# Hybrid retention and differential attention on one core: attention in one step per product, a fixed rotation of raw weight slots, and two weight sums made by adding DMAs

## The chip, the cores and the metric

The kernel runs on 1 core of one Trainium2 chip. The metric is the device time of one execution in microseconds; a kernel's time is the median of its runs. Engines are named as the profile names them: PE (TensorE, matmuls), DVE (VectorE), ACT (ScalarE), POOL (GpSimd) and SP (SyncE, which here only issues DMAs). L813 means line 813 of the kernel's file. One execution of each kernel is recorded by the hardware profiler; all rows below come from it.

## The reference, cut to what matters

```python
u = rms_norm(h, g_norm)                      # h: 16 meta tokens + 512 tokens, D_MODEL 2048
proj = u @ w_in                              # 2048 x 8192, float32
rq, rk, rv, rgate, dq, dk, dv, dgate = jnp.split(proj, offs, axis=-1)
# 8 heads of each kind, 128 wide
r = retention(rq, rk, rv, valid)             # chunk-causal, decay by distance
r = head_layer_norm(r, g_ret) * jax.nn.silu(rgate)
d = diff_attention(dq, dk, dv, valid, lam)   # softmax(q0 k0) - lam * softmax(q1 k1), then v
d = head_rms_norm(d, g_diff) * (1.0 - lam_init) * jax.nn.silu(dgate)
y = jnp.concatenate([r, d], axis=-1) @ w_out # 2048 x 2048
return rms_norm(h + y, final_norm_g)
```

All of it is float32. The kernel splits each float32 operand in a high and a low part and makes one product of three matmuls (high x high, high x low, low x high).

## The kernel before

**Stages.** From 0 to about 100 us the rows of x are normed and transposed and the first six column groups are projected one by one. From about 100 to 806 us the other 58 column groups of w_in are projected two at a time, in 29 pairs such as (dv, dk) or (rq, rg) of one head, and the attention of the heads runs between them. From 806 us on the output projection and the last norm follow.

**A pair and its seven products.** A pair takes two column groups ka and kb, the 2048 rows of w_in in two halves, and the tokens in two halves. That is a 2 x 2 block product, done with seven block products P1 to P7 in place of eight, which needs sums of raw weight pieces. A raw piece is 128 x 1024 float32, 512 KB: b11 and b21 are the two halves of ka, b12 and b22 those of kb. `ORDER` is P3, P7, P1, P6, P2, P5, P4. Each product needs its piece split: ACT casts it to `wh` (L785), DVE makes `wl` from it (L796); both are prepared two products ahead, with three buffers each. PE then runs 24 matmuls (L813). Between the splits four sums per pair are made in the raw pieces, two on DVE (L799, L801) and two on POOL (L803, L804). PSUM banks p3, v, x, y collect the products; ACT copies p3, v and x out of three rotating banks (`snap`, L825) and DVE adds (L829).

**Attention in steps.** `ret_task` (retention of a head) and `diff_task` (differential attention of a head) are generators; `step()` takes every task in the list one `yield` further, and `run_pair` calls it at chosen places between the products. A diff task takes, for four query blocks and two softmaxes, scores (PE, L590, L596), score plus distance and row maximum (DVE, L604), the maximum times the slope (L606), the exponential (ACT, L607), and combines the two (L613 to L616); then transposes (PE, L629), splits and the product with v. ACT loads its table anew when it goes from SiLU to the exponential or back (ACT_TABLE_LOAD). A step of the retention is one block of scores s_r, times the decay table (L552), split (L556, L557), and one block back its product with v, `o_r` (L526 to L528).

**The end of a head, `finish`.** The head's rows get a norm factor in hops: squares, one matmul `ms` (PE, L463), a copy of its first row (ACT, L464), a DMA of that row to a column `mc` (SP, L467), four small POOL instructions (L469 to L472), a DMA to DRAM `rd` (L474) and a broadcast back into `sq` (L476); then DVE multiplies the head `oc` by it (L479), by the gain and the SiLU gate (L480), and the head is split into `mxh` and `mxl` and both are written to DRAM (L490), to be read back before the output projection.

**What sets the order.** A pass that places instructions before the run fixes each engine's order; engines then run their lists in order and wait at semaphores, and SP and POOL do so for the DMAs they issue as well. Heads 1 to 6 take their pairs in the order (rv, rk), (rq, rg), (dv, dk), (dq, dg); head 7 takes dv, dk and dq, dg first. Raw pieces come from a pool of five buffers (`wr`), loaded by SP in w_in's own layout, 512-byte rows.

Of the kernel before, what the change touches and what calls it, by code (L numbers as in the profile page):

```python
# [15 lines left out]
P = 128  # L16
# [23 lines left out]
def hymba_kernel(ctx: ExitStack, tc: tile.TileContext, x, meta, norm_g, w_in, w_out, g_ret, g_diff,  # L40
# [14 lines left out]

    def pj(name):
        return ps.tile([P, 512], F32, tag="pj", bufs=3, name=name)
# [85 lines left out]
    mt = ap.tile([4 * META, 512], F32, tag="s2k", bufs=3, name="mt")  # L143
# [304 lines left out]
    def finish(po, col, T, gate, nm):  # L448
        oc = ap.tile([P, L], F32, tag="s2k", bufs=3, name=f"oc_{nm}")[:, :SEQ]
        vec.tensor_scalar(oc, po, OMAX, -OMAX, op0=ALU.min, op1=ALU.max)  # L450

        sq = ap.tile([P, L], F32, tag="s2k", bufs=3, name=f"sq_{nm}")[:, :SEQ]
        sr = ap.tile([P, L], F32, tag="s2k", bufs=3, name=f"sr_{nm}")[:, :SEQ]
# [13 lines left out]
        nc.sync.dma_start(out=mc, in_=sq[0:1, :].rearrange("o (p j) -> o p j", j=4))  # L467
        rc = sm.tile([P, 4], F32, tag="rc", name=f"rc_{nm}")
# [4 lines left out]
        rd = dr.tile([P, 4], F32, tag="rd", name=f"rd_{nm}")  # L473
        nc.sync.dma_start(out=rd, in_=rc)  # L474
        bc = sq
        nc.sync.dma_start(out=bc, in_=rd.rearrange("p j -> (p j)").rearrange("(o n) -> o n", o=1)  # L476
                          .broadcast_to([P, SEQ]))
        yield
        vec.tensor_tensor(out=oc, in0=oc, in1=bc, op=ALU.mult)  # L479
        vec.scalar_tensor_tensor(oc, oc, gcol[:, col:col + 1], T[gate], op0=ALU.mult, op1=ALU.mult)  # L480
        if col in heads_mix:
            hi, lo = heads_mix[col]
        else:
            hi, lo = (ap.tile([P, SEQ], F32R, tag="r2k", bufs=4, name=f"mx{t}_{nm}") for t in "hl")
        act.copy(out=hi, in_=oc)  # L485
        vec.tensor_tensor(out=lo, in0=oc, in1=f(hi), op=ALU.subtract)
        if col not in heads_mix:
            spilled[col] = dr.tile([P, 2, SEQ], F32, tag=f"mx{col}", bufs=1, name=f"mx{col}")
            for j, t in enumerate((hi, lo)):
                nc.sync.dma_start(out=spilled[col][:, j, :], in_=f(t))  # L490
# [38 lines left out]

    def ret_task(h, T):  # L530
        nm = f"r{h}"
        tab = ap.tile([P, 576], F32, tag="tab", name=f"tab{h}")
        nc.sync.dma_start(out=tab, in_=decay_tab[h])
        vh, vl = v_rows(T["rv"], nm, True)
# [3 lines left out]
        state["scores"] = state.get("scores", 0) + 5  # L538
        t0s = [0, 64, 192, 320, 448]
        prev = None  # L540
        for i in range(6):
            if i < 5:
# [8 lines left out]
                pf = ap.tile([P, L], F32, tag="s2k", bufs=3, name=f"pf_{nm}_{i}")  # L551
# [22 lines left out]
    def diff_task(h, T):  # L574
        nm = f"d{h}"
        vh, vl = T["d_rows"] if "d_rows" in T else v_rows(T["dv"], nm, False)
        slope = 2.0 ** -(h + 1)
        state["scores"] = state.get("scores", 0) + 4
        aa = []
        for b in range(4):  # L580
            w = 2 * 72 + P * b
            zz = sm.tile([P, 2], F32, tag="zz", name=f"zz_{nm}_{b}")
            pp = []

            for s in range(2):
# [26 lines left out]
            rr = sm.tile([P, 2], F32, tag="rr", name=f"rr_{nm}_{b}")
            vec.reciprocal(rr, zz)  # L613
            vec.tensor_tensor(out=rr[:, 1:2], in0=rr[:, 1:2], in1=neglam, op=ALU.mult)
            vec.tensor_scalar(pp[1], pp[1], rr[:, 1:2], None, op0=ALU.mult)  # L615
            vec.scalar_tensor_tensor(pp[0], pp[0], rr[:, 0:1], pp[1], op0=ALU.mult, op1=ALU.add)  # L616
            aa.append(pp[0])
            yield

# [75 lines left out]
    def put_dk(src):  # L695

        a = kbuf[0]
        for (d1, cols), (d2, _) in zip(*(both_parts(a[:, i, :]) for i in range(2))):
            act.copy(out=d1, in_=src[:, :, cols])
            vec.tensor_tensor(out=d2, in0=src[:, :, cols], in1=f(d1), op=ALU.subtract)  # L700
        return spread_dk()

    def spread_dk():
        a, b = kbuf
        for rows in (slice(0, DH), slice(DH, P)):
            nc.sync.dma_start(out=f(b[rows]), in_=f(a[DH:]))
        nc.sync.dma_start(out=f(a[DH:]), in_=f(a[:DH]))
        return [(t[:, 0, :], t[:, 1, :]) for t in kbuf]
# [15 lines left out]
    def sums_of_u():  # L724
# [3 lines left out]
        for k in range(0, 8, 2):  # L728
# [7 lines left out]
            def out(i, t):  # L736
                act.copy(out=sums[i][0][:, sl, :], in_=t)
                vec.tensor_tensor(out=sums[i][1][:, sl, :], in0=t, in1=f(sums[i][0][:, sl, :]), op=ALU.subtract)

            c = whole("fc", [t[k // 4] for t in uc], slice(k % 4, k % 4 + 2), "s2k", 3)  # L740
            d = whole("fd", ud, sl, "s2k", 3)
            vec.tensor_tensor(out=d, in0=c, in1=d, op=ALU.add)
            out(1, d)
# [44 lines left out]
    def prepare_lo(i):  # L788
# [27 lines left out]
    def run_pair(n, T):  # L816
# [38 lines left out]
        if keys:  # L855
            step()
# [11 lines left out]
        step()  # L868
        run(5, y, True)
# [3 lines left out]
        if ka in ("rq", "dq"):  # L873
# [3 lines left out]
            act.activation(T[kb], T[kb], AF.Silu)  # L877
        else:
# [3 lines left out]
            if kb == "rk":  # L882
                T[kb] = [kbuf[0][:, i, :] for i in range(2)]
                for (d1, cols), (d2, _) in zip(*(both_parts(t) for t in T[kb])):
                    act.activation(d1, s37[:, :, cols], AF.Copy, scale=K_SCALE)
                    vec.scalar_tensor_tensor(d2, s37[:, :, cols], K_SCALE, f(d1), op0=ALU.mult, op1=ALU.subtract)
            else:
                T[kb] = put_dk(s37)
        run(6, v, True)

        if keys:
            for d, cols in key_parts(vT, 1):
                add(d, su2[:, cols], v[:, cols])
# [43 lines left out]
    load_pair(0)  # L937
# [13 lines left out]
    prepare_hi(0)
    prepare_lo(0)
    prepare_hi(1)
    prepare_lo(1)
# [13 lines left out]
    for ks in kpairs:  # L968
        for k in list(range(KT))[ks]:
            if k in spilled:  # L970
                for j, t in enumerate(heads_mix[k]):
                    nc.sync.dma_start(out=f(t), in_=spilled[k][:, j, :])

# [146 lines left out]
```

## Time and profile before

| | us |
|---|---|
| median of 3 runs | 1033.93 (1033.39 to 1037.14) |
| the profiled execution, its own time | 1036.45 |
| its span in the trace | 1034.4 |
| PE busy | 964.7 (93% of the span) |
| DVE busy | 824.0 (80%) |
| ACT busy | 538.7 (52%) |
| POOL busy | 242.7 (23%) |
| DMA queue of SP, share of the 16 DMA engines | 42.2% |

The time is the whole execution; the span runs from the first to the last instruction of the trace, 2.05 us less here. Busy shares are means over stages that differ: a window of the span tells which engine works and which waits there.

### The profile page before, as it was taken

How to read it: one execution, taken by the hardware profiler on the slowest of the kernel's cores; microseconds unless marked ns; L12 is line 12 of the kernel's file. 1: busy time of each engine (PE TensorE's matmuls, PEld its weight loads, DVE VectorE, ACT ScalarE, POOL GpSimd, SP SyncE). 2: the span in 40 equal slices, each digit the busy share in tenths (PEclk: the TensorE clock that was granted, in tenths of full speed). 3: DMA queues.
4: the chain of work that ended last, by engine and by line, in shares of the span. 5: the costliest groups of instructions: out<-in, count | busy, mean ns of one | idle time of the engine just before them, and what ended most of it. 6: DMA issues, size and time to landing. Idle time of an engine off the chain costs nothing.

```text
span 1034.4 us, 18382 instructions
## 1 busy us (share of the span) xinstructions
PE 964.7 (93%) x7215; PEld 921.6 (89%) x7215; DVE 824.0 (80%) x1332; ACT 538.7 (52%) x979; POOL 242.7 (23%) x169
## 2 busy tenths in 40 slices
PE   6999988999999999899999999999994999799997
PEld 6999988999999999899999999999983988588896
DVE  6698869899989998999899989989996754334432
ACT  6454565565656564646565656565654443223322
POOL 4453131132233213321332133233220200000001
PEclk8999999999999999999999999999997999999998
DMA  9512533353235334543643264226443496143304
GB/s 269 158 43 73 125 93 103 82 155 114 82 97 152 107 109 116 139 121 87 140 134 98 82 156 113 83 82 156 113 113 102 161 385 212 50 126 96 122 1 163
DMA packets 166405, 127.03 MB, mean 123 GB/s; under 512 B 9712, under 2 KB 145008, under 8 KB 165808
## 3 DMA queue, kind: packets, MB, share of 16 engines
q1 hardware_dynamic: 165744, 124.04, 42.2%
q10 hardware_dynamic: 576, 1.84, 0.5%
q8 instruction: 56, 0.92, 0.4%
q14 instruction: 29, 0.24, 0.1%
HBM read 107.77 MB, written 11.57 MB: 115 GB/s over the span
## 4 chain that ended last, share of the span: by engine, by line
PE 54%; DVE 21%; DMA 9%; issue 6%; POOL 6%; ACT 4%; SPq 0%; POOLq 0%; DVEq 0%; ACTq 0%
PE y L526 6%; PE y L527 5%; PE y L528 5%; DVE wl_P L796 5%; PE y_rqrg L813 4%; PE x_dvdk L813 3%; PE x_dqdg L813 3%; DMA mc_r<-sq_r 2%; PE x_rqrg L813 2%; PE y_dvdk L813 2%; PE v_rqrg L813 2%; DMA sq_r<-rd_r 2%; PE v_dvdk L813 2%; DVE p_d L615 2%; PE y_rvrk L813 2%
## 5 line engine op out<-in xcount | busy, mean ns | idle before, releaser
L785 ACT CAST wh_P<-b 128x1024 fp32r<-128x1024 f32 x203 | 212.7, 1049 | 147.9 <-DVE mx_d L606 30.3
L796 DVE TENSOR_TENSOR wl_P<-b,wh_P 128x1024 fp32r<-128x1024 f32 x203 | 260.3, 1284 | 13.0 <-ACT wh_P L785 11.0
L803 POOL TENSOR_TENSOR b<-b,b 128x1024 f32<-128x1024 f32 x29 | 69.9, 2412 | 406.1 <-DVE b L799 301.7
L104 DVE TENSOR_TENSOR wl<-wr,wh 128x1024 fp32r<-128x1024 f32 (+1 forms) x40 | 49.8, 1252 | 69.3 <-ACT wh L103 69.2
L804 POOL TENSOR_TENSOR b<-b,b 128x1024 f32<-128x1024 f32 x29 | 76.8, 2649 | 105.5 <-DVE wl_P L796 32.5
L103 ACT CAST wh<-wr 128x1024 fp32r<-128x1024 f32 (+1 forms) x40 | 40.8, 1029 | 88.7 <-PE y L528 70.1
L607 ACT ACTIVATE p_d<-p_d,mx_d 128x144 f32<-128x144 f32 (+3 forms) x64 | 36.6, 572 | 31.7 <-DVE mx_d L606 31.1
L799 DVE TENSOR_TENSOR b<-b,b 128x1024 f32<-128x1024 f32 x29 | 35.5, 1223 | 0.6
L629 PE MATMUL at_d<-ident,p_d 128*128 128x128 f32 (+1 forms) x112 | 23.1, 275 | 13.3 <-DVE p_d L616 12.9
L801 DVE TENSOR_TENSOR b<-b,b 128x1024 f32<-128x1024 f32 x29 | 35.2, 1214 | 0.1
L813 PE MATMUL x_dqdg<-uah,wh_P 128*128 128x256 f32 x128 | 32.2, 290 | 3.0 <-ACT s_dqdg L825 3.0
L1049 POOL TENSOR_SCALAR rs<-ssq,pre 128x1 f32<-128x1 f32 x4 | 1.9, 486 | 136.1 <-ACT jk L1007 136.1
L813 PE MATMUL x_dqdg<-ual,wh_P 128*128 128x256 f32 x128 | 31.2, 282 | 0.0
L526 PE MATMUL y<-wh,mix_s3h 128*128 128x512 f32 (+1 forms) x64 | 23.6, 382 | 6.3 <-ACT mix_s3h L485 5.1
L813 PE MATMUL x_dvdk<-uah,wh_P 128*128 128x264 f32 x112 | 28.5, 284 | 0.0
L813 PE MATMUL x_dvdk<-ual,wh_P 128*128 128x264 f32 x112 | 28.4, 284 | 0.0
L813 PE MATMUL x_rvrk<-uah,wh_P 128*128 128x264 f32 x112 | 28.4, 285 | 0.0
L813 PE MATMUL x_rvrk<-ual,wh_P 128*128 128x264 f32 x112 | 28.2, 285 | 0.0
L629 PEld LDWEIGHTS at_d<-ident,p_d 128*128 128x128 f32 (+1 forms) x112 | 12.8, 126 | 17.3 <-DVE p_d L616 14.8
L813 PEld LDWEIGHTS x_dqdg<-uah,wh_P 128*128 128x128 f32 x128 | 24.1, 188 | 4.2 <-ACT s_dqdg L825 4.2
L526 PE MATMUL y<-wh,mix_s2h 128*128 128x512 f32 (+1 forms) x80 | 27.8, 348 | 0.0
L528 PE MATMUL y<-wh,mix_al 128*128 128x512 f32 (+1 forms) x80 | 27.8, 348 | 0.0
(567 smaller groups left out, 3550.5 us busy)
## 6 DMA issues: line engine op xcount, KB each, us to landing
b<-in_w_in_dram SPq DMA_DIRECT2D x116, 512.0 KB, 4.6
wr<-in_w_out_dram SPq DMA_DIRECT2D x32, 512.0 KB, 4.1
kbuf<-kbuf SPq DMA_DIRECT2D x24, 264.0 KB, 4.9
wr<-in_w_in_dram SPq DMA_DIRECT2D x12, 512.0 KB, 8.5
tab<-in_decay_tab_dram SPq DMA_DIRECT2D x8, 288.0 KB, 4.3
sq_r<-rd_r SPq DMA_DIRECT2D x8, 256.0 KB, 3.6
sq_d<-rd_d SPq DMA_DIRECT2D x8, 256.0 KB, 4.2
mx<-mxh_r SPq DMA_DIRECT2D x7, 256.0 KB, 3.7
```

Source lines behind the costliest of these rows:

```text
L103: act.copy(out=hi, in_=raw)
L104: eng.tensor_tensor(out=lo, in0=raw, in1=f(hi), op=ALU.subtract)
L526: pe.matmul(o, ah, bh, start=start, stop=False)
L527: pe.matmul(o, ah, bl, start=False, stop=False)
L528: pe.matmul(o, al, bh, start=False, stop=stop)
L607: act.activation(p, p, AF.Exp, bias=mx, scale=slope, accum_out=zz[:, s:s + 1])
L629: pe.transpose(at[:n, b * P - q0:(b + 1) * P - q0], aa[b][:, kc:kc + n], ident)
L785: act.copy(out=hi, in_=raw_w[n][SOURCE[pn]])
L796: vec.tensor_tensor(out=lo, in0=w[SOURCE[pn]], in1=f(hi), op=ALU.subtract)
L803: pool.tensor_tensor(out=w["b12"], in0=w["b12"], in1=w["b11"], op=ALU.subtract)
L804: pool.tensor_tensor(out=w["b11"], in0=w["b21"], in1=w["b22"], op=ALU.subtract)
L813: pe.matmul(o, w_[:, kt, :], u[lo][:, kt, c0:], start=not add and w_ is wh and kt == 0 and lo == 0, stop=w_ is wl and kt == 7, skip_group_ ...
```

## The change

- **Pairs.** Heads 1 to 7 all take (dv, dk), (dq, dg), (rv, rk), (rq, rg), so the retention of a head runs beside the next head's dv, dk and dq, dg, and the diff attention beside its own head's rv, rk and rq, rg. `ORDER` ends P4, P5; P4 goes to the bank of v. The three PSUM banks are chosen by name.
- **Steps.** One `step()` per product, in `run` itself (two in pair 1 and the first three products of pair 2). `finish` has seven more yields; the combining of a diff block comes one block later, and its scaling by the second softmax's factor goes from DVE to ACT. The maximum is taken as a minimum of the negated scores, so L606's multiplication goes. Rows of v and the copies of k are tasks of their own.
- **Weights.** w_in is laid out on the host so that a piece is one contiguous block. Five raw slots rotate by a fixed table. Per pair five plain loads (t, b22, b11, b21, t1; t1 is b11's data again) and two adding DMAs from POOL: t += half 1 of kb, t1 += half 0 of kb. DVE makes t += b11 behind P7's split and t += b21 behind P6's. POOL's sums go. Signs are folded into the sums of u, the scale of SiLU and that of k.
- **Spilled heads.** They are written whole, in one DMA, and split when they are read back.

```diff
-    ORDER = ("P3", "P7", "P1", "P6", "P2", "P5", "P4")
+    ORDER = ("P3", "P7", "P1", "P6", "P2", "P4", "P5")
...
-        ps_ = ps_[3:] if h == 0 else ps_[2:] + ps_[:2] if h == HEADS - 1 else ps_
+        ps_ = ps_[3:] if h == 0 else ps_[2:] + ps_[:2]
...
-        if pn == "P3":
-            vec.tensor_tensor(out=w["b22"], in0=w["b22"], in1=w["b12"], op=ALU.subtract)
-        elif pn == "P7":
-            vec.tensor_tensor(out=w["b22"], in0=w["b22"], in1=w["b11"], op=ALU.add)
-        elif pn == "P1":
-            pool.tensor_tensor(out=w["b12"], in0=w["b12"], in1=w["b11"], op=ALU.subtract)
-            pool.tensor_tensor(out=w["b11"], in0=w["b21"], in1=w["b22"], op=ALU.subtract)
+        if pn == "P7":
+            vec.tensor_tensor(out=w["t"], in0=w["t"], in1=w["b11"], op=ALU.add)
+        elif pn == "P6":
+            vec.tensor_tensor(out=w["t"], in0=w["t"], in1=w["b21"], op=ALU.add)
...
+    slots = [{"t": 0, "b22": 1, "b11": 2, "b21": 3, "t1": 4}]
+    for n in range(len(pair_list)):
+        p_ = slots[n]
+        slots.append({"t": p_["b22"], "b22": p_["b11"], "b11": p_["b21"], "b21": p_["t"], "t1": p_["t1"]})
...
+    def loads(n, j):
+        m = n + 1
+        if j == 0:
+            more(n, "t1", 0)
+        elif j == 1:
+            more(m, "t", 1)
+            load(m, "b22")
+        elif j == 3:
+            load(m, "b11")
+        elif j == 4:
+            load(m, "b21")
+        elif j == 5:
+            load(m, "t1")
+        elif j == 6:
+            load(m + 1, "t")
+    def more(n, b, half):
+        if n < len(pair_list):
+            h, _, kb = pair_list[n]
+            pool.dma_start(out=raw_w[n][b].rearrange("p (k n) -> p k n", n=P), in_=w_piece(kb, h, half), accum_op=ALU.add)
+    SOURCE = {"P7": "t", "P3": "b22", "P1": "b11", "P6": "t", "P2": "b21", "P5": "t1", "P4": "t"}
...
         def run(j, o, more=False):
+            loads(n, j)
             prepare_hi(i0 + j + 2)
             prepare_lo(i0 + j + 2)
+            step()
+
+            if n == 1 or n == 2 and j < 3:
+                step()
             product(i0 + j, o, keys, more)
...
+        def combine(b, zz, pp):
+            rr = sm.tile([P, 2], F32, tag="rr", name=f"rr_{nm}_{b}")
+            vec.reciprocal(rr, zz)
+            vec.tensor_tensor(out=rr[:, 1:2], in0=rr[:, 1:2], in1=neglam, op=ALU.mult)
+            act.activation(pp[1], pp[1], AF.Copy, scale=rr[:, 1:2])
+            yield
+            vec.scalar_tensor_tensor(pp[0], pp[0], rr[:, 0:1], pp[1], op0=ALU.mult, op1=ALU.add)
+            aa.append(pp[0])
...
-                vec.tensor_tensor_reduce(shape(p), shape(dist[:, 384 - P * b:]), sp, op0=ALU.add, op1=ALU.max,
-                                         scale=1.0, scalar=-3e38, accum_out=mx)
-                vec.tensor_scalar(mx, mx, -slope, None, op0=ALU.mult)
-                act.activation(p, p, AF.Exp, bias=mx, scale=slope, accum_out=zz[:, s:s + 1])
+                vec.tensor_tensor_reduce(shape(p), shape(dist[:, 384 - P * b:]), sp, op0=ALU.add, op1=ALU.min,
+                                         scale=-slope, scalar=3e38, accum_out=mx)
+                act.activation(p, p, AF.Exp, bias=mx, scale=-1.0, accum_out=zz[:, s:s + 1])
...
+        yield
+        yield
         rc = sm.tile([P, 4], F32, tag="rc", name=f"rc_{nm}")
...
         rd = dr.tile([P, 4], F32, tag="rd", name=f"rd_{nm}")
+        yield
         nc.sync.dma_start(out=rd, in_=rc)
+        yield
         bc = sq
...
         yield
+        yield
         vec.tensor_tensor(out=oc, in0=oc, in1=bc, op=ALU.mult)
```

POOL's list before, in head 2 (`b` are raw pieces, `rc` and `mc` a head's norm factor):

```order
L804 TENSOR_TENSOR b_7_3256<-b_7_3258,b_7_3252 128x1024
L803 TENSOR_TENSOR b_8_3589<-b_8_3589,b_8_3591 128x1024
L469 TENSOR_SCALAR rc_d_3644<-mc_d_3642 128x4
L470 TENSOR_TENSOR rc_d_3644<-rc_d_3644,mhalf 128x4
L471 TENSOR_SCALAR mc_d_3642<-mc_d_3642 128x4
L472 TENSOR_TENSOR rc_d_3644<-rc_d_3644,mc_d_3642 128x4
L804 TENSOR_TENSOR b_8_3591<-b_8_3593,b_8_3587 128x1024
```

and after, in head 1 (`t_3` is t1 of pair 3, the other two are t and t1 of pair 4):

```order
L835 DMA t_3_2155<-in_w_in_dram 128x1024
L835 DMA t_2191<-in_w_in_dram 128x1024
L479 TENSOR_SCALAR rc_d_2019<-mc_d_1982 128x4
L480 TENSOR_TENSOR rc_d_2019<-rc_d_2019,mhalf 128x4
L481 TENSOR_SCALAR mc_d_1982<-mc_d_1982 128x4
L482 TENSOR_TENSOR rc_d_2019<-rc_d_2019,mc_d_1982 128x4
L835 DMA t_4_2469<-in_w_in_dram 128x1024
```

The sums of 128x1024 are gone; an adding DMA stands at most of their places, and a head's factor still stands between two of them.

DVE's list before, where the diff attention of heads 6 and 7 meet (`oc_d` is head 6, the scores and the gate `sg` head 7):

```order
L616 SCALAR_TENSOR_TENSOR p_d_2_0_9746<-p_d_2_0_9746,rr_d_2_9759,p_d_2_1_9754 128x400
L479 TENSOR_TENSOR oc_d_9732<-oc_d_9732,sq_d_9734 128x512
L604 ISA p_d_3_1_9863,mx_d_3_1_9864<-dist,s_d_3_1_9858 128x528
L604 ISA mx_d_3_1_9864 128x1
L480 SCALAR_TENSOR_TENSOR oc_d_9732<-oc_d_9732,gcol,sg_dg_8943 128x512
L606 TENSOR_SCALAR mx_d_3_1_9864<-mx_d_3_1_9864 128x1
L829 TENSOR_TENSOR sg_dg_9564<-s_dqdg_9438,s_dqdg_9335 128x256 x2
```

and after, where those of heads 0 and 1 meet:

```order
L601 SCALAR_TENSOR_TENSOR p_d_1_0_2291<-p_d_1_0_2291,rr_d_1_2333,p_d_1_1_2299 128x272
L492 TENSOR_TENSOR oc_d_1918<-oc_d_1918,sq_d_1920 128x512
L631 ISA p_d_2_1_2349,mx_d_2_1_2350<-dist,s_d_2_1_2346 128x400
L631 ISA mx_d_2_1_2350 128x1
L631 ISA p_d_3_0_2396,mx_d_3_0_2397<-dist,s_d_3_0_2391 128x528
L631 ISA mx_d_3_0_2397 128x1
L493 SCALAR_TENSOR_TENSOR oc_d_1918<-oc_d_1918,gcol,sg_dg_1555 128x512
L597 RECIPROCAL rr_d_2_2386<-zz_d_2_2337 128x2
L885 TENSOR_TENSOR sg_dg_2223<-s_dqdg_2081,s_dqdg_1959 128x256 x2
```

The multiplication that waits for the broadcast of the earlier head stands ahead of the later head's scores and gate in both; the heads are 0 and 1 now, and in heads 6 and 7 it no longer does.

DVE's list before, where head 3's diff attention ends:

```order
L440 TENSOR_TENSOR p_str<-pf_r_4_6130,p_str 16x64
L796 TENSOR_TENSOR wl_P_6295<-b_16_6061,wh_P_6293 128x1024
L479 TENSOR_TENSOR oc_d_6007<-oc_d_6007,sq_d_6009 128x512
L480 SCALAR_TENSOR_TENSOR oc_d_6007<-oc_d_6007,gcol,sg_dg_5232 128x512
L450 TENSOR_SCALAR oc_r_6282<-o_r_5973 128x512
```

and after:

```order
L571 TENSOR_TENSOR pl_r_1_5449<-pf_r_1_5446,ph_r_1_5448 128x448
L492 TENSOR_TENSOR oc_d_5242<-oc_d_5242,sq_d_5244 128x512
L885 TENSOR_TENSOR su_dvdk_5480<-s_dvdk_5427,pj_dvdk_5429 128x264
L855 TENSOR_TENSOR wl_P_5486<-t_13_5236,wh_P_5484 128x1024
L566 TENSOR_TENSOR pf_r_2_5493<-s_r_2_5489,tab_5391 128x320
```

Before, the retention's last score block is already behind DVE when the multiplication comes; after, it stands between the second and the third block of the retention (`pl_r_1`, `pf_r_2`) of the same head, beside the next head's (dv, dk).

## Rows read from the trace of the kernel before

**Rows 1.** The page's first part: busy us, share, instructions of PE.

```profile
PE 964.7 (93%) x7215; PEld 921.6 (89%) x7215; DVE 824.0 (80%) x1332; ACT 538.7 (52%) x979; POOL 242.7 (23%) x169
```

**Rows 2.** Windows of the span: length, busy us of each engine, granted clock, DMA.

```profile
0.00:200.00 200.00, 181.24 (x1424) 175.33 (x1425) 160.98 (x277) 109.43 (x213) 64.03 (x51) 0.98 0.43 121
200.00:700.00 500.00, 482.17 (x3882) 473.33 (x3881) 472.23 (x747) 299.88 (x538) 141.01 (x86) 1.00 0.43 113
700.00:781.00 81.00, 76.58 (x623) 75.01 (x622) 77.61 (x129) 48.04 (x89) 21.67 (x11) 1.00 0.52 131
781.00:806.00 25.00, 10.25 (x51) 8.47 (x50) 12.84 (x36) 8.99 (x19) 1.85 (x4) 0.66 0.25 76
786.80:803.80 17.00, 6.41 (x27) 5.71 (x27) 6.63 (x20) 6.12 (x13) 0.32 (x2) 0.50 0.23 69
```

**Rows 3.** Waits of PE from 200 to 700 us: total, times, longest.

```profile
PE at_d L629 <- DVE p_d L616: 6.7, 5, 2.0
PE s_d L590 <- DVE mx_d L604: 5.3, 4, 1.4
PE x_dqdg L813 <- ACT s_dqdg L825: 2.6, 3, 1.4
```

**Rows 4.** Timeline of the last head: start, length, engine, [idle before, releaser].

```profile
782.02 0.47 PE L463 MATMUL ms_d<-sh_d,ones 128*128 128x512 f32 x1 [0.77 <-DVE mx_d L604]
...
793.61 0.69 DVE L479 TENSOR_TENSOR oc_d<-oc_d,sq_d 128x512 f32<-128x512 f32 x1 [4.37 <-DMA sq_d<-rd_d]
...
796.99 1.28 ACT L877 ACT_TABLE_LOAD   x1
...
799.23 0.59 PE L813 MATMUL y_rvrk<-s2h,wh_P 128*128 128x264 f32 x1 [9.34 <-ACT s_rvrk L825]
799.62 0.42 PE L813 MATMUL y_rvrk<-s2l,wh_P 128*128 128x264 f32 x1
799.84 0.42 PE L813 MATMUL y_rvrk<-s2h,wh_P 128*128 128x264 f32 x1
```

**Rows 5.** POOL's second sum by line (busy, mean ns), and one in the timeline.

```profile
L804 POOL TENSOR_TENSOR b<-b,b 128x1024 f32<-128x1024 f32 x29 | 76.8, 2649 | 105.5 <-DVE wl_P L796 32.5
...
771.55 2.40 POOL L804 TENSOR_TENSOR b<-b,b 128x1024 f32<-128x1024 f32 x1 [5.18 <-DVE wl_P L796]
771.78 2.44 DVE L693 SCALAR_TENSOR_TENSOR dq_h<-su_dqdg,dq_h 64x256 fp32r<-64x256 f32 x1
774.26 0.42 DVE L693 SCALAR_TENSOR_TENSOR dq_l<-su_dqdg,dq_l 64x256 fp32r<-64x256 f32 x1
```

**Rows 6.** Groups of instructions by line: busy us, mean ns | idle before.

```profile
L796 DVE TENSOR_TENSOR wl_P<-b,wh_P 128x1024 fp32r<-128x1024 f32 x203 | 260.3, 1284 | 13.0 <-ACT wh_P L785 11.0
...
L606 DVE TENSOR_SCALAR mx_d<-mx_d 128x1 f32<-128x1 f32 x64 | 8.3, 147 | 0.2
...
L877 ACT ACT_TABLE_LOAD x7 | 9.0, 1283 | 0.1
```

**Rows 7.** Timeline of PE inside one product, at the full clock.

```profile
442.66 0.28 PE L813 MATMUL y_rvrk<-s1h,wh_P 128*128 128x264 f32 x1
442.79 0.28 PE L813 MATMUL y_rvrk<-s1l,wh_P 128*128 128x264 f32 x1
```

**Rows 8.** DMA issues: queue, count, KB each, median us to landing.

```profile
b<-in_w_in_dram SPq DMA_DIRECT2D x116, 512.0 KB, 4.6
...
wr<-in_w_in_dram SPq DMA_DIRECT2D x12, 512.0 KB, 8.5
...
hr_dh<-in_x_dram SPq DMA_DIRECT2D x1, 1024.0 KB, 16.2
...
mc_r<-sq_r SPq DMA_DIRECT2D x8, 2.0 KB, 4.1
```

**Rows 9.** Timeline in a head whose finish runs beside POOL's sums.

```profile
395.12 0.39 PE L463 MATMUL ms_d<-sh_d,ones 128*128 128x512 f32 x1
...
410.28 0.69 DVE L479 TENSOR_TENSOR oc_d<-oc_d,sq_d 128x512 f32<-128x512 f32 x1 [2.08 <-DMA sq_d<-rd_d]
```

More of the change, by code (lines that the diff above doesn't have):

```diff
@@ L54, in f @@
         return t.bitcast(F32)
+    state = {"n": 0, "pieces": 0, "ring": -1, "scores": 0, "pj": -1}
     def pj(name):
-        return ps.tile([P, 512], F32, tag="pj", bufs=3, name=name)
+        state["pj"] = (state["pj"] + 1) % 3
+        return ps.tile([P, 512], F32, tag=f"pj{state['pj']}", name=name)
     def pm(name):
@@ L481, in finish @@
         if col in heads_mix:
-            hi, lo = heads_mix[col]
+            split(oc, *heads_mix[col])
         else:
[L484 to L490, printed above, removed]
+            spilled[col] = dr.tile([P, SEQ], F32, tag=f"mx{col}", bufs=1, name=f"mx{col}")
+            yield
+            nc.sync.dma_start(out=spilled[col], in_=oc)
     def v_rows(vT, nm, centre):
@@ L611, in diff_task @@
             state["scores"] -= 1
[L612 to L617, printed above, removed]
+            late = (b, zz, pp)
             yield
+        for _ in combine(*late):
+            pass
+        yield
         tiles = [(META, 0, 0, 4), (P, 16, 0, 0), (P, 144, P, 1), (P, 272, 2 * P, 2), (P, 400, 3 * P, 3)]
@@ L661, in scores_done @@
     def scores_done():
-        while state.get("scores", 0):
+        while state["scores"]:
             step()
@@ L698, in put_dk, with spread_task @@
         for (d1, cols), (d2, _) in zip(*(both_parts(a[:, i, :]) for i in range(2))):
[L699 to L703, printed above, removed]
+            act.activation(d1, src[:, :, cols], AF.Copy, scale=-1.0)
+            vec.scalar_tensor_tensor(d2, src[:, :, cols], -1.0, f(d1), op0=ALU.mult, op1=ALU.subtract)
+        tasks.append(spread_task())
+        return [(t[:, 0, :], t[:, 1, :]) for t in kbuf]
+    def spread_task():
         a, b = kbuf
@@ L706, in spread_dk @@
             nc.sync.dma_start(out=f(b[rows]), in_=f(a[DH:]))
+        yield
+        yield
         nc.sync.dma_start(out=f(a[DH:]), in_=f(a[:DH]))
-        return [(t[:, 0, :], t[:, 1, :]) for t in kbuf]
     def project(pi, keys, nm, between):
@@ L734, in whole, with out @@
                 return t
[L736 to L743, printed above, removed]
+            def out(i, t, sign=1.0):
+                hi, lo = (x[:, sl, :] for x in sums[i])
+                act.activation(hi, t, AF.Copy, scale=sign)
+                vec.scalar_tensor_tensor(lo, t, sign, f(hi), op0=ALU.mult, op1=ALU.subtract)
+            c = whole("fc", [t[k // 4] for t in uc], slice(k % 4, k % 4 + 2), "f0")
+            d = whole("fd", ud, sl, "f1")
+            vec.tensor_tensor(out=d, in0=c, in1=d, op=ALU.subtract)
+            out(1, d, -1.0)
             yield
@@ L751, in sums_of_u @@
             out(3, c)
-            vec.tensor_tensor(out=a2, in0=a2, in1=d, op=ALU.subtract)
-            out(4, a2)
+            vec.tensor_tensor(out=a2, in0=a2, in1=d, op=ALU.add)
+            out(4, a2, -1.0)
             yield
@@ L867, in run_pair @@
             (put_rq(T[ka], 0, x) if ka == "rq" else put_dq(T[ka], 0, x, h))
-        step()
-        run(5, y, True)
+        run(5, v, True)
+        if keys:
+            for d, cols in key_parts(vT, 1):
+                add(d, su2[:, cols], v[:, cols])
+        else:
+            add(su2, su2, v)
+            (put_rq(T[ka], 1, su2) if ka == "rq" else put_dq(T[ka], 1, su2, h))
+        run(6, y, True)
         su25 = s1
@@ L936, in hymba_kernel @@
             act.copy(out=d, in_=outs[half][:, cols])
-    load_pair(0)
+    for b in slots[0]:
+        load(0, b)
     outs = project(10, True, "dk0", sums_on)
@@ L947, in hymba_kernel @@
             vec.tensor_tensor(out=d2, in0=outs[half][:, cols], in1=f(d1), op=ALU.subtract)
-    T["dk"] = spread_dk()
+    T["dk"] = [(t[:, 0, :], t[:, 1, :]) for t in kbuf]
+    tasks.append(spread_task())
+    T["r_rows"] = v_rows(T["rv"], "r0", True)
     T["d_rows"] = v_rows(T["dv"], "d0", False)
     tasks.append(ret_task(0, T))
[L951 to L954, printed above, removed]
+    state["scores"] += 5
+    more(0, "t", 1)
+    for i in range(2):
+        prepare_hi(i)
+        prepare_lo(i)
+    load(1, "t")
     for n in range(len(pair_list)):
@@ L967, in hymba_kernel, with fetch @@
             heads_mix[k] = [t[:, j, :] for t in hl]
[L968 to L972, printed above, removed]
+    fetched = set()
+    def fetch(upto):
+        for i in range(min(upto, len(kpairs))):
+            ks = [k for k in list(range(KT))[kpairs[i]] if k in spilled]
+            if i not in fetched and ks:
+                t = raw_slot(f"mb{i}")
+                for j, k in enumerate(ks):
+                    nc.sync.dma_start(out=t[:, j * SEQ:j * SEQ + SEQ], in_=spilled[k])
+                for j, k in enumerate(ks):
+                    split(t[:, j * SEQ:j * SEQ + SEQ], *heads_mix[k])
+            fetched.add(i)
+    fetch(2)
     state["pieces"] = len(pieces)
```

97 lines of the change are left out of this document (50 added, 47 removed).

## The prediction

> **What bounds the kernel now.** I read the busy times first, then the windows, then the waits of the engine that the windows point to. TensorE (PE) is busy for 964.7 of the 1034.4 us [rows 1]. VectorE (DVE) is the only engine near it, and only in the seven heads: from 200 to 700 us PE is busy 482.2 and DVE 472.2 of 500 [rows 2]. So the time can fall only where PE stands still or is clocked down, and the difference of window and busy time places that: 18.8 us in 0 to 200, 17.8 in 200 to 700, 4.4 in 700 to 781, 14.8 in 781 to 806, and what is left of the span's 69.7 (1034.4 - 964.7), 14.0, after that. The change removes no matmul (7216 before, 7216 after), so 69.7 us plus what the clock costs is the most it can win.
>
> The list of PE's waits says what ends them in the heads [rows 3]: nearly all are in differential attention, where PE waits for DVE to finish a probability block (6.7 us) or a score bank (5.3), or for ScalarE (ACT) to empty a bank (2.6). The 25 us from 781 to 806 are one event, in the last head [rows 4]. The row mean `ms_d` leaves PE at 782.02; ACT copies it, SP sends it, POOL makes the factor, SP sends that out and back, and DVE, which stands in order at L479, goes on at 793.61: 11.6 us after `ms_d`. Behind that DVE instruction stand the SiLU input of the same engine, ACT's table load at 796.99 and ACT's bank copy, so PE gets its next product at 799.23, 17.2 us after `ms_d`, with 9.34 idle at a stretch. From 786.8 to 803.8 the granted clock is 0.50, the lower of its two levels (1.2 of 2.4 GHz), behind a stretch in which PE hardly worked [rows 2].
>
> **The change part by part.** *POOL's sums become adding DMAs.* 58 sums go; the second of each pair's two takes 2.65 us [rows 5]. They also hold DVE: while POOL ran one from 771.55 for 2.40 us, a DVE instruction on 64x256 took 2.44, and its like right after 0.42. A meeting costs DVE 2.0 us; 58 at most are 116 us, 16 in a head of four pairs (8 x 2.0), less where they miss. DVE keeps two weight sums per pair, and loses 64 multiplications of 147 ns [rows 6] and the 32 scalings of L615, which go to ACT. So DVE should fall from 94% in the heads to some 80 to 84%. ACT gets the scalings, and 16 more table loads of 1.283 us, 20.5 us in all, beside a busy share of 60% [rows 2, 6]: hidden while one load, 1.3 us, is shorter than a product (24 matmuls 0.12 us apart, 2.9 us [rows 7]), and ACT works two products ahead.
>
> *What the adding DMAs cost.* No row shows one. For t1 the addition is issued beside a pair's first product and the sum is split beside its fifth, so four products, 4 x 2.9 = 11.6 us, lie between, and two more products before PE uses it; t has five. Bounds: a plain load of a 512 KB weight piece lands after 4.6 us; the slowest weight loads of the page take 8.5, and the slowest load of all, 1024 KB in a crowd of others, 16.2 [rows 8]. With 4.6 to 8.5 it is hidden, cost 0; at 16.2 it would be some 1.4 to 4.6 us late in each pair. I take 0, since the first row is the same size and source. POOL issues in order: an addition behind one of the 16 finishes waits for its `mc`, which lands 4.1 us after issue [rows 8], still inside 11.6. The plain loads that replace the strided ones (now whole rows of 4 KB, five per pair for four) sit on SP with the finishes' hops; each waits for the last read of its slot, at most a product, 2.9 us. This may lengthen a finish's three hops, and is in the upper bound of the next term.
>
> Here a row and a rule speak against the change. The row is POOL and DVE holding each other for 2.4 us [rows 5]. The Trainium skill, "SBUF — State Buffer", section "Who interferes with whom", goes further: a DMA seen to stall beside a DVE instruction is one issued by GpSimd, whose descriptors could not be written meanwhile. If a hold lasts one DVE instruction (1.28 us for the commonest, [rows 6]), the landing goes to 5.9 or 9.8 us and the sum stays; if it lasts through DVE's unbroken work, that is the third rival. No run here shows it yet.
>
> *Heads 2 to 6, 17.8 us of idle PE.* The diff blocks now stand one per product, their combining a block later, so PE reads a block that DVE finished a product ago; I walk these blocks to 0.4 us of stall per head. A new spot arises: DVE's L492 (the old L479) of the diff head stands in the next head's retention, ahead of the sum and the score block that PE's `o_r` needs. PE gets from `ms_d` to that `o_r` in 4.5 products and 3 us of scores (13.6 us by the order); DVE needs 2.6 us from L492 on (a sum, a split of 1.28, a score block, and its cast on ACT). With the hops at 11.6 us (the event above) PE waits 0.6; with 15.2 (395.12 to 410.28, a head with POOL's sums in the way [rows 9]) 4.2. I take 1.3, near the first, as the sums are gone. Five heads: 5 x (1.3 + 0.4) = 8.5, so **-9.3**; ends -15 and +6.
>
> *The last head's event.* The order no longer lets two diff heads meet there. It lets them meet at head 1: between `ms_d0` and the fourth product of (rv, rk) 1 stand half a product and the scores of d1, about 5 us of work, and on DVE and ACT the same chain (L492, scores, SiLU input, table load, bank copy). By the same rows it is 17.2 us long: 12 idle, and the lower clock again. So 14.8 + 2.4 (a product there takes 24 x 0.22 = 5.3 for 2.9 [rows 4, 7]) becomes 12 + 2.4: **-2.8**; ends -17 (no gap there) and +3.
>
> *The rest.* 700 to 781: 4.4 us of the same diff waits, to 1.7: **-2.7**. 0 to 200: quicker loads and no POOL sums against a denser pair 1: **-3**; ends -7 and +4. After 806 nothing but the spilled heads' reading (one copy, split again by ACT and DVE, which there are half idle): **0**, plus or minus 1.5.
>
> **Sum.** -9.3 -2.8 -2.7 -3 = -17.8. The profiled execution took 1036.45 us (span 1034.4 and 2.05 around it); it would be 1018.6. It lies 2.5 above the median of 1033.93, so the median forecast is **1016**.
>
> **The rivals.** *The gap closes wholly*: DVE, without the locks, gets to L492 late enough or the hops early enough that neither the five heads nor head 1 stop. Then 12 + 2.4 + 6.5 = 20.9 more is won: 995. For it speaks DVE's new room; against it, the chain at head 1 is hop after hop and has no work beside it.
>
> *The finish stops every head*: same work, but the hops now wait for steps and for SP's loads; at 15.2 us and above, PE stops some 5 us in five heads instead of 1.3, 18.5 more: 1034, no change. For it: the hops took 15.2 in [rows 9], and DVE stood there idle for 2.08 of it already; the steps spread them further. Against: POOL no longer has a sum of 2.65 us [rows 5] ahead of the factor.
>
> *The additions come late* (slower): POOL's descriptors or the read-add-write delay them past 11.6 us and the two products' reserve; then PE stops once or twice in each of 29 pairs. The point from which it decides is a stall of 0.6 us per pair (17.8 / 29). At 2 us per pair it is 58 us: 1016 + 58 = 1074; it can be anything from 1034. For it: nothing here has ever timed such a DMA, and there are 58, one every 14 us; against: 4.6 us for the same bytes without the sum.
>
> **Chances.** Forecast 0.46; gap closes 0.18; finish stops 0.20; additions late 0.16. A measurement of this kernel tells 0.5% from no change, 5.2 us: 1028.8 and 1039.1 are the marks. Faster: 0.46 + 0.18 and a little of the third, 0.66. Same: most of the third and the fringe, 0.17. Slower: 0.17. The range leaves out the far end of the first rival and most of the last: 997 to 1042.
>
> **What would show it.** The additions: landing of the DMA issues under POOL; below 11 us and no PE wait on the cast of t1 is right. The locks: the DVE group of 64x256 at one duration, about 0.42, and DVE near 84% in the heads. The diff waits: PE's `at_d` and `s_d` lines under 3 us from 200 to 700. The moved event: a PE gap of 10 to 13 us near 190 to 250 us with clock 0.5 behind it, none near 790. The new spot: an `o_r` line of PE of some 6 us in five pieces, and DVE's waits at L492. Wrong would be a PE wait on weights in every pair, or a mean head as long as before.

## The result and the profile after

The changed kernel takes 1063.91 us (median of 4 runs, 1063.38 to 1066.96) against 1035.54 for the kernel before beside it: a ratio of 1.028, 95% interval 1.0246 to 1.0313. It is slower, by some 28 us; 1016 was forecast, in a range of 997 to 1042. The profiled execution has a span of 1062.1 us against 1034.4.

The page's busy times, and the DMA queues of the changed kernel (q0 is the new one, of the adding DMAs; name, packets, MB, share of the 16 engines), which answer to [rows 1]:

```profile
PE 976.9 (92%) x7215; PEld 936.9 (88%) x7215; DVE 720.6 (68%) x1236; ACT 572.8 (54%) x1027; POOL 138.0 (13%) x169
...
q1 hardware_dynamic: 51200, 131.90, 40.0%
q0 software_dynamic: 8352, 30.41, 16.3%
```

DVE fell by 103 us and POOL by 105, yet PE is busy 12.2 us longer for the same matmuls, and idle for 85.2 us where it was 69.7. The windows (columns as in [rows 2]) place both; 200 to 919 holds the pairs from the middle of head 1 on and, from 862, the first part of the output projection:

```profile
0.00:200.00 200.00, 175.61 (x1375) 169.84 (x1375) 151.72 (x272) 112.09 (x222) 52.62 (x56) 0.97 0.57 158
200.00:919.00 719.00, 671.41 (x5096) 652.47 (x5096) 515.13 (x885) 421.25 (x738) 81.23 (x105) 0.96 0.63 167
919.00:1062.00 143.00, 129.85 (x744) 114.57 (x744) 53.76 (x80) 39.43 (x69) 4.18 (x8) 0.96 0.28 94
```

Idle is 24.4 us up to 200 (18.8 before), 47.6 up to 919 (37.0 from 200 to 806 before, and none from there to 890), 13.2 behind (14.0 before). The pairs of the kernel before end at 835 us, not at 806 as its stages were given; that moves no idle time. What PE waits for from 200 to 920 us (answers to [rows 3]), and what DVE waits for in the whole span:

```profile
PE s_d L616 <- DVE mx_d L631: 28.8, 6, 5.1
PE o_r L535 <- ACT ph_r L570: 11.8, 5, 3.1
PE s_d L622 <- DVE mx_d L631: 4.7, 1, 4.7
PE o_r L536 <- DVE pl_r L571: 4.1, 2, 3.7
...
DVE oc_r L492 <- DMA sq_r<-rd_r: 57.9, 8, 11.5
DVE oc_d L492 <- DMA sq_d<-rd_d: 44.3, 8, 6.8
```

In heads 1 to 6 PE stops twice each: some 4.8 us at a score block of the diff attention (`s_d`), and 2.1 to 3.7 us at the retention's `o_r`. Both waits lead back to DVE, which is itself held at L492, the multiplication behind the broadcast of a finish: 102 us in all, where the same line held DVE for 33 us before. The `s_d` stop comes from the retention's finish, the `o_r` stop from that of the diff attention. One retention finish, with the stop that it makes (start, length, engine, [idle before, releaser]; other rows lie between these):

```profile
386.02 0.39 PE L471 MATMUL ms_r<-sh_r,ones 128*128 128x512 f32 x1
387.28 0.52 SPq L475 DMA_DIRECT2D mc_r<-sq_r  x1
392.61 1.02 POOL L479 TENSOR_SCALAR rc_r<-mc_r 128x4 f32<-128x4 f32 x1 [17.12 <-DMA mc_r<-sq_r]
396.16 0.33 SPq L485 DMA_DIRECT2D rd_r<-rc_r  x1
399.45 0.33 SPq L488 DMA_DIRECT2D sq_r<-rd_r  x1
...
404.76 0.69 DVE L492 TENSOR_TENSOR oc_r<-oc_r,sq_r 128x512 f32<-128x512 f32 x1 [6.87 <-DMA sq_r<-rd_r]
405.37 0.75 DVE L885 TENSOR_TENSOR sg_dg<-s_dqdg,s_dqdg 128x256 f32<-128x256 f32 x2
406.04 0.30 DVE L631 CUSTOM_DVE_ANT_0 p_d<-dist,s_d 128x144 f32<-128x144 f32 x1
406.40 1.03 PE L616 MATMUL s_d<-kbuf,dq_h 128*128 128x400 f32 x2 [4.53 <-DVE mx_d L631]
```

The three DMA hops take 5 + 3 + 5 us and the whole way 18.7 us. In [rows 9] it was 15.2, but that is a diff head's finish; the retention's took 14.6 in the mean before. DVE was at L492 already 11.9 us after `ms_r`. Behind it stand the diff attention's first blocks, and PE's next score block needs the bank that one of them empties. Each of the six `s_d` stops is followed by 6.8 us at the lower clock, for instance:

```profile
302.50:309.30 6.80, 5.63 (x23) 5.63 (x24) 6.63 (x17) 5.78 (x11) 0.00 (x0) 0.50 0.58 121
404.90:411.70 6.80, 5.30 (x22) 5.29 (x23) 6.63 (x15) 5.49 (x11) 0.00 (x0) 0.50 0.59 148
```

There are six of them, one per head, and 13.6 us more at 193 to 207, in the event of head 1. Of the six `o_r` stops only the two longest (3.7 and 3.1 us) are followed by one, of 3.4 us; the four of 2.1 to 2.4 us are not.

### The profile page after: what moved, and what is told of

The parts are those of the page before. It is cut to its first block, busy times and chain, and to the rows that moved or that the text cites. A ratio compares the mean times of both kernels' runs of the same rounds, so it can differ in the third digit from the quotient of the medians.

```text
span 1062.1 us, 18466 instructions
## 1 busy us (share of the span) xinstructions
PE 976.9 (92%) x7215; PEld 936.9 (88%) x7215; DVE 720.6 (68%) x1236; ACT 572.8 (54%) x1027; POOL 138.0 (13%) x169
## 3 DMA queue, kind: packets, MB, share of 16 engines
q1 hardware_dynamic: 51200, 131.90, 40.0%
q0 software_dynamic: 8352, 30.41, 16.3%
## 4 chain that ended last, share of the span: by engine, by line
PE 62%; DMA 20%; POOL 6%; DVE 5%; ACT 3%; issue 2%; SPq 1%; POOLq 0%; DVEq 0%; ACTq 0%
PE pj_rqrg L869 13%; PE pj_rvrk L869 11%; PE pj_dqdg L869 9%; PE pj_dvdk L869 6%; PE y L535 5%; PE y L536 4%; PE y L537 4%; DMA sq_r<-rd_r 4%; DMA mc_r<-sq_r 3%; DMA sq_d<-rd_d 3%; DMA mc_d<-sq_d 2%; DMA rd_d<-rc_d 2%; DMA rd_r<-rc_r 2%; PE pj_rk L295 1%; PE at_d L655 1%
## 5 line engine op out<-in xcount | busy, mean ns | idle before, releaser
L844 ACT CAST wh_P<-t 128x1024 fp32r<-128x1024 f32 x116 | 121.6, 1048 | 78.3 <-PE pj_rvrk L869 20.6
L855 DVE TENSOR_TENSOR wl_P<-t,wh_P 128x1024 fp32r<-128x1024 f32 x116 | 141.4, 1219 | 7.0 <-ACT wh_P L844 4.2
L844 ACT CAST wh_P<-b 128x1024 fp32r<-128x1024 f32 x87 | 91.4, 1051 | 56.7 <-issue 14.3
L855 DVE TENSOR_TENSOR wl_P<-b,wh_P 128x1024 fp32r<-128x1024 f32 x87 | 106.2, 1221 | 22.2 <-ACT wh_P L844 21.3
L835 POOL DMA_DIRECT2D t<-in_w_in_dram x58 | 51.6, 890 | 472.0 <-DMA t<-in_w_in_dram 207.7
L633 ACT ACTIVATE p_d<-p_d,mx_d 128x144 f32<-128x144 f32 (+3 forms) x64 | 36.8, 575 | 15.5 <-DVE mx_d L631 14.6
L492 DVE TENSOR_TENSOR oc_r<-oc_r,sq_r 128x512 f32<-128x512 f32 x8 | 5.5, 692 | 57.9 <-DMA sq_r<-rd_r 57.9
L858 DVE TENSOR_TENSOR t<-t,b 128x1024 f32<-128x1024 f32 x29 | 35.4, 1222 | 0.5
L492 DVE TENSOR_TENSOR oc_d<-oc_d,sq_d 128x512 f32<-128x512 f32 x8 | 5.5, 693 | 44.3 <-DMA sq_d<-rd_d 44.3
L869 PE MATMUL pj_rvrk<-ual,wh_P 128*128 128x264 f32 x112 | 35.5, 337 | 0.0
L869 PE MATMUL pj_rvrk<-uah,wh_P 128*128 128x264 f32 x112 | 35.5, 337 | 0.0
L860 DVE TENSOR_TENSOR t<-t,b 128x1024 f32<-128x1024 f32 x29 | 35.3, 1216 | 0.3
L869 PE MATMUL pj_dqdg<-uah,wh_P 128*128 128x256 f32 x128 | 31.2, 282 | 0.6 <-DVE kbuf L1008 0.6
L869 PE MATMUL pj_dqdg<-ual,wh_P 128*128 128x256 f32 x128 | 31.1, 281 | 0.0
```

The costliest lines, as they stand in the source:

```text
L633: act.activation(p, p, AF.Exp, bias=mx, scale=-1.0, accum_out=zz[:, s:s + 1])
L835: pool.dma_start(out=raw_w[n][b].rearrange("p (k n) -> p k n", n=P), in_=w_piece(kb, h, half), accum_op=ALU.add)
L844: act.copy(out=hi, in_=raw_w[n][SOURCE[pn]])
L855: vec.tensor_tensor(out=lo, in0=w[SOURCE[pn]], in1=f(hi), op=ALU.subtract)
L858: vec.tensor_tensor(out=w["t"], in0=w["t"], in1=w["b11"], op=ALU.add)
L860: vec.tensor_tensor(out=w["t"], in0=w["t"], in1=w["b21"], op=ALU.add)
```

## The experiments

Two theories, to be told apart first. **A, the place:** the pass that fixes the order put L492 far ahead of where it is written (the code has eight steps between the splitting `sh` and L492, one product each; in DVE's list three weight splits lie between them in the diff finish of head 3), so DVE gets there before the broadcast can have landed, and everything behind it waits. **B, the traffic:** the hops got longer because of the adding DMAs. Beside them stand C, that the new order of pairs is the cause, and D, that the additions themselves are late. Single runs are marked as such; the kernel before, run beside them, took 1033.2 to 1041.8 us in 14 runs.

**e1_pin: L492 at its written place.** The function orders the instruction behind what was written before it on its engine, and adds no wait.

```diff
-        vec.tensor_tensor(out=oc, in0=oc, in1=bc, op=ALU.mult)
+        tc.keep_in_program_order(vec.tensor_tensor(out=oc, in0=oc, in1=bc, op=ALU.mult))
```

> Edit: the changed kernel, with the one DVE instruction that waits for the broadcast of a finish (L492) kept behind everything written before it, which moves it some 16 rows down DVE's list in heads 1 to 6. Theory A (its place): DVE stood there 102 us and PE lost 49 us to s_d and o_r behind it, and some 12 us more to the lower clock after each stop; all of that goes, 1002 to 1018 us, and the six stretches of 6.8 us at half clock go too. Theory B (the hops got long because of the added DMA traffic): the place helps only by what it is later, the hops stay at 19 us, some 1040 to 1055. Theory D (the adding DMAs are late themselves): no change, 1055 to 1065.

1006.98 us (4 runs, 1006.28 to 1007.16), a ratio of 0.9709 to the kernel before (0.9676 to 0.9742): 57 us less than the changed kernel, by an edit to the place of one instruction per finish. In head 3 it now stands here in DVE's list, behind `p_str`, the retention's last block (to be held against the place that the section on the change shows):

```
L447 TENSOR_TENSOR p_str<-pf_r_4_5586,p_str 16x64
L885 TENSOR_TENSOR s_dvdk_5427<-s_dvdk_5427,pj_dvdk_5429 128x264
L855 TENSOR_TENSOR wl_P_5630<-b_14_5430,wh_P_5628 128x1024
L492 TENSOR_TENSOR oc_d_5242<-oc_d_5242,sq_d_5244 128x512
```

The `o_r` stops are gone. What is left of DVE's and PE's waits at these places:

```profile
DVE oc_r L492 <- DMA sq_r<-rd_r: 32.9, 8, 7.7
...
PE s_d L622 <- DVE mx_d L631: 12.6, 6, 4.4
```

The six stretches of 6.8 us at the lower clock are gone (clock 0.99 from 200 to 862 us; one of 3.4 us is left). So A holds and D falls: with 58 adding DMAs running as before, no wait of PE, ACT or DVE is for one. The broadcast still lands 20.5 us after `ms` in the retention's finishes, as B said of the hops.

**e2_noadd: no adding DMAs,** at the places that the pass chose.

```diff
-            pool.dma_start(out=raw_w[n][b].rearrange("p (k n) -> p k n", n=P), in_=w_piece(kb, h, half), accum_op=ALU.add)
+            pass
```

> Edit: the changed kernel without its 58 adding DMAs; the two weight sums that they make are left out, so t and t1 hold half of what they should. Everything else runs as before. Theory A: the retention's hops shorten by 1 to 2 us of 19, DVE still stands at L492, 1045 to 1060. Theory B: hops back to 15 us and less, waits at L492 halved, 1030 to 1042. Theory D: the largest fall, to 1016 or below, since nothing is late any more.

1034.26 us (one run): 30 us less, with L492 not kept in place (DVE is there even earlier, 10.1 us after `ms` for 11.9 in the retention's finishes). That is B's forecast, and A alone missed it. The time from `ms` to the landing of the broadcast falls from 19 to 14 us in the retention's finishes, though the five plain loads per pair and the finish's added steps are still there: neither of them had made it long. The waits:

```profile
PE o_r L535 <- ACT ph_r L570: 11.1, 5, 2.5
PE s_d L616 <- DVE mx_d L631: 10.0, 7, 4.2
...
DVE oc_d L492 <- DMA sq_d<-rd_d: 40.9, 8, 6.2
DVE oc_r L492 <- DMA sq_r<-rd_r: 39.0, 8, 11.6
```

The `s_d` stops fall to a third, but the `o_r` stops stay. The diff attention's finishes, behind which these stand, were hardly lengthened by the adding DMAs: in heads 1 to 6 the broadcast lands 13.8 us after `ms` in the kernel before, 13.5 in the changed one and 12.9 here, while DVE gets to the line after 12.1, 7.5 and 7.5. So the traffic makes the `s_d` stops long, and the `o_r` stops come from DVE's early arrival. Over all, each theory alone is refuted by the other's run: a stop is the landing less DVE's arrival, the place moved the one and the adding DMAs the other.

**e5_plain: the adding DMAs as plain copies,** on the same queue, with the same bytes.

```diff
-            pool.dma_start(out=raw_w[n][b].rearrange("p (k n) -> p k n", n=P), in_=w_piece(kb, h, half), accum_op=ALU.add)
+            pool.dma_start(out=raw_w[n][b].rearrange("p (k n) -> p k n", n=P), in_=w_piece(kb, h, half))
```

> Edit: the changed kernel with the 58 adding DMAs made plain copies on the same queue, same bytes from the same source; the two weight sums are left out (t and t1 hold the copied piece alone). Theory B1 (it is the adding that holds the DMA engines: in the changed kernel the adding queue takes 16.3% of them for 30 MB, 3.0 us of all 16 per 512 KB, where a plain load of these rows takes 1.3): the retention's finishes go from 19 us back to 13 to 15 and the time to 1034 to 1044. Theory B2 (any 512 KB more per sum, or the software queue itself): they stay at 17 to 19 us, 1050 to 1062.

1031.18 us (one run), with retention finishes of 15.2 us: B1, though the time came out 3 us below its range and the finishes just above theirs. The queue's line:

```profile
q0 software_dynamic: 8352, 30.41, 9.6%
```

The same packets and bytes took 16.3% of the engines when they added: 16.3% of 1062.1 us over 58 DMAs is 3.0 us of all 16 engines each, and 9.6% of 1029.4 is 1.7 us. By the same reckoning SP's queue took 1.7 us per 512 KB in the changed kernel (40.0% for 131.90 MB), where the expectation had 1.3 for a plain load. It is the adding that is dear, not the 30 MB.

**e3_mcact: the first hop on another queue.**

```diff
-        nc.sync.dma_start(out=mc, in_=sq[0:1, :].rearrange("o (p j) -> o p j", j=4))
+        act.dma_start(out=mc, in_=sq[0:1, :].rearrange("o (p j) -> o p j", j=4))
```

> Edit: the changed kernel with the first hop of each finish (mc) issued from ACT's queue, right behind ACT's copy, and not from SP's, where weight loads stand ahead of it. Theory B in its form 'the hop queues behind loads on the same queue': the landing of mc_r goes from 4.9 to some 2.5 us, and each of the retention's finishes gets 2 to 4 us shorter; at some 12 stops that is 15 to 25 us, 1038 to 1050. If the length is that of the whole memory path and not of one queue: landing as before, 1055 to 1064. Theory A says nothing of the hop, but agrees with any fall.

1058.64 us (one run), in the range of the second reading; `mc_r` lands 4.3 us after its issue, not 2.5. The form of B in which a hop stands behind loads in one queue is refuted for the larger part: on a queue of its own it is nearly as slow. That all queues share the 16 engines would fit this, and was not tested further.

**e4_order: the pairs of heads 1 to 6 in the order of before,** (rv, rk) first.

```diff
-        ps_ = ps_[3:] if h == 0 else ps_[2:] + ps_[:2]
+        ps_ = ps_[3:] if h == 0 else ps_[2:] + ps_[:2] if h == HEADS - 1 else ps_
```

> Edit: the changed kernel with the pairs of heads 1 to 6 in the order of before: (rv, rk), (rq, rg), (dv, dk), (dq, dg). Theory C (the new order of pairs is the cause, as it puts the end of the retention ahead of the diff attention's first score blocks): the s_d waits of 28.8 us go, 1030 to 1042. Theory A: DVE stands at L492 as long, other work behind it is hit, 1050 to 1070.

1055.9 us (one run), and the stops stay:

```profile
PE s_d L616 <- DVE mx_d L631: 33.4, 6, 7.0
PE o_r L535 <- ACT ph_r L570: 12.1, 5, 4.2
...
DVE oc_r L492 <- DMA sq_r<-rd_r: 54.4, 8, 9.4
DVE oc_d L492 <- DMA sq_d<-rd_d: 40.2, 8, 7.9
```

C falls: in either order of the pairs, work stands behind L492.

**e7_pinr: only the retention's finishes at their written place.**

```diff
-        vec.tensor_tensor(out=oc, in0=oc, in1=bc, op=ALU.mult)
+        ins = vec.tensor_tensor(out=oc, in0=oc, in1=bc, op=ALU.mult)
+        if gate == "rg":
+            tc.keep_in_program_order(ins)
```

> Edit: the changed kernel with L492 kept in its written place for the retention's finishes alone; those of the diff heads stay where the scheduler put them. Theory A by parts: the s_d stops (33.5 us of idle PE) and the half-clock stretches behind them go, the o_r stops (16 us) stay: 1015 to 1025. If the two stops feed each other: 1030 or above, or the o_r stops grow past 20 us.

1032.22 us (one run), 7 above the range of "by parts" and in that of "the two stops feed each other". The s_d stops of the six heads are gone, as forecast; the other kind did not stay at 16 us but grew:

```profile
PE o_r L538 <- DVE pl_r L573: 19.3, 6, 3.8
```

and stretches of 3.4 to 6.8 us at the lower clock now follow five of these six stops (2.7 to 3.8 us long), where they followed two of six in the changed kernel. Taken in this order the two kinds of finish are worth some 32 and some 25 us (1063.9 to 1032.2 to 1007.0), but as the `o_r` stops grew, the parts do not simply add; why they grew was not tested.

**e8_later: as e1_pin, and one step more** before L492 in the retention's finishes of heads 1 to 6 (and in the diff finish of head 0).

```diff
-        vec.tensor_tensor(out=oc, in0=oc, in1=bc, op=ALU.mult)
+        if gate == "rg" and 0 < int(nm[1:]) < HEADS - 1:
+            yield
+        if nm == "d0":
+            yield
+        tc.keep_in_program_order(vec.tensor_tensor(out=oc, in0=oc, in1=bc, op=ALU.mult))
```

> Edit: as e1_pin, and one step more ahead of L492 in the retention's finishes of heads 1 to 6 and in the diff finish of head 0. Theory A carried on: the 12.6 us of s_d stops that e1_pin still has come from DVE standing at L492 for 2 to 5 us in these heads, so they fall under 5 us and the time to 996 to 1003. If what is left in e1_pin is no matter of the place: 1004 to 1009.

998.61 us (4 runs, 996.96 to 999.99), a ratio of 0.9648 to the kernel before (0.9633 to 0.9662): the fastest version here. Its window that holds as many matmuls as 200 to 919 in the changed kernel:

```profile
200.00:859.00 659.00, 651.53 (x5096) 635.95 (x5096) 516.05 (x892) 420.25 (x738) 77.13 (x105) 0.99 0.69 183
```

The same 5096 matmuls take 659 us for 719: 40.1 us less idle (7.5 for 47.6) and 19.9 us less busy. Nearly all of the latter is the clock (0.99 for 0.96): in these windows PE worked 41.0 us at half clock in the changed kernel and 4.9 here, and half of the difference is 18. From 207 to 854 us PE does not stand at all; 4.3 of the 7.5 us are the wait at the output projection, which begins at 854.7 here and at 918.1 in the changed kernel. The step in head 0's finish shows no gain: DVE is at L492 8.4 us after `ms` there in all three kernels, and head 1's stop of 4.6 us stays.

**e9_latermc: e8_later with the first hop from ACT's queue** (the edits of e3_mcact and e8_later together).

> Edit: as e8_later, with the first hop of each finish issued from ACT's queue. With the place right the length of a hop no longer matters: the same as e8_later within 3 us. If the hops still end last somewhere: 3 to 8 us faster than e8_later.

1002.94 us (4 runs, 1000.22 to 1005.95). No faster, and in the median 4.3 us slower, 1.3 more than the expectation allowed, which the runs do not explain (the two profiled spans are alike, 998.4 and 998.2, but they are this kernel's fastest run and e8_later's slowest). The broadcast landed 18.9 us after `ms` in the retention's finishes of heads 1 to 6 instead of 21.5, with DVE there after 20.9: hops that were 2.6 us shorter gained nothing.

**The two sides of a stop.** For the six retention finishes of heads 1 to 6, in the mean, from the start of the matmul `ms` in the trace: when the broadcast has landed, and when DVE gets to the line (the start of the multiplication less DVE's idle time before it). Where DVE gets there later than the landing it does not wait.

| kernel | landed, us | DVE there, us | time, us |
|---|---|---|---|
| before | 14.6 | 14.4 | 1035.5 |
| changed | 19.0 | 11.9 | 1063.9 |
| e2_noadd | 14.1 | 10.1 | 1034.3 |
| e5_plain | 15.2 | 11.9 | 1031.2 |
| e4_order | 19.8 | 11.8 | 1055.9 |
| e1_pin | 20.5 | 16.9 | 1007.0 |
| e8_later | 21.5 | 21.0 | 998.6 |

In the fastest version the broadcast lands latest of all. From the kernel before to the changed one DVE also gets there earlier; whether that is its list alone, or also that it has less to do, was not separated.

## Why the prediction was wrong

- **The weight sums by DMA (cost 0): right for what waits for them, wrong for what they pass.** They land after 5.4 to 9.9 us, 6.5 in the median, inside the 11.6 that I had; PE waits for none. The issues on POOL (shortest, median and longest in ns) and the landings:

```profile
L835 POOL DMA_DIRECT2D t<-in_w_in_dram x58: 853/874/1080, 81.5 to 835.7; - x58
...
DMA to landing us min/median/max: 5.4/6.5/9.9
```

  Their bound was drawn for their own landing only. That they would take the DMA engines for 3.0 us each, and so lengthen the retention's finishes by 4 to 5 us (19.0 against 15.2 with plain copies and 14.1 with none), was no term of the sum.
- **The locks: right; DVE's share was put too high.** The DVE instructions on 64x256 that write `dq_h` now take 0.41 to 0.42 us each. DVE is busy 72% from 200 to 919 and 78% in the shorter window of e8_later, for 80 to 84 said. I had set against the change that a DMA seen to stall beside a DVE instruction is one issued by GpSimd (the Trainium skill, "SBUF — State Buffer", section "Who interferes with whom"). No such stall is seen here: the issue on POOL took 853 to 1080 ns in all 58.
- **Heads 2 to 6 (-9.3, ends -15 and +6): the step that failed.** I had found the new spot, L492 of the diff head ahead of the retention's `o_r`. Its mechanism was right and its price too low by about half: 2.1 to 3.1 us in each of the five heads for 1.3, with the broadcast landing after 12.7 to 13.7 us and 3.1 us of work behind it, not 2.6. (PE gets from `ms_d` to that `o_r` in 13.7 us, the 13.6 of the sum; but 4.5 products of 2.9 us and 3 us of scores, as I described that way, would be 16.1.) The other kind of finish I had not looked at: the retention's own L492, ahead of the diff attention's scores, on blocks that I had walked as 0.4 us. It cost 4.5 to 5.1 us in each of six heads. PE gets from `ms_r` to that score block in 15.9 us and DVE needs 1.6 from L492 on, so at a landing of 15.2, the most that I took, the stop would be 0.9 us, and at the 19.0 measured it is 4.7. The blocks' own waits went as I said: the `at_d` line of [rows 3], 6.7 us, is gone from 200 to 920. And I gave the clock to the event of the two diff heads alone: behind the other stops it cost about half as much again as the idle time (19.9 beside 40.1 us).
- **The last head's event moves to head 1: right.** Near 790 there is no gap; at 190 to 203 the gaps are 0.4, 1.3, 1.5, 4.7 and 1.8 us, 9.7 for the 12 said, though in five pieces and not in one, with 13.6 us at the lower clock.
- **0 to 200 us: -3 said, and about that measured.** The window shows +5.6, but 8 us of head 1's event lie before 200 and belong to the term above. At 190.1 us, where that event begins, PE has started 1369 matmuls and stood 16.3 us; the kernel before has started 1371 at 193 us and stood 18.8: -2.4. Behind 919 the idle time is 13.2 us for 14.0, with 0 said.
- **The rivals.** "The finish stops every head" named the mechanism and put it at 1034 with 0.20: one stop of 5 us in five heads, without the clock; there were two a head. "The gap closes wholly" (995) is nearly reached by e8_later (998.6), once one instruction per finish stands where it is written and a step later, though head 1 still stops there. The additions were not late.

## What to carry to other kernels

When an instruction waits for a chain of DMAs on an in-order engine, look at its place in that engine's list, not at where the code has it: an ordering pass can put it far ahead of that place, and then steps written in between are lost (why this pass did so is not shown). Size such a stop as landing less arrival, for every finish in the kernel and with the new traffic in the landing; a change that moves the arrival forward can make the stop as well as one that delays the landing. And count the clock with the stops, not only the idle time.

## What the runs showed of the hardware

An adding DMA of 512 KB took the 16 engines 3.0 us where the same copy on the same queue took 1.7 and landed after 4.8 us instead of 6.5; beside the adding DMAs the three hops of a retention finish landed after 4.9, 2.0 and 5.8 us (medians), without them after 3.7, 1.4 and 4.7. In the changed kernel all six PE stops of 4.5 to 5.1 us in an otherwise full stretch were followed by 6.8 us at half the clock (0.50 granted), and two of the six of 2.1 to 3.7 us by 3.4 us; together the stops cost about half as much again as their idle time. The length of a stop alone did not tell: in e1_pin one of 2.0 us was followed by 3.4 us at half the clock, and one of 3.1 us was not.
